# The last MLP block by chunks of 384 tokens, with each chunk's tail behind it, in a two-layer hybrid trunk

## The chip, the cores and the metric

The kernel runs on one core of one Trainium2 chip. Its engines are TensorE (PE in the rows, with its weight loads as PEld), VectorE (DVE), ScalarE (ACT), GpSimd (POOL) and SyncE (SP), whose queue issues the DMA transfers. The metric is the device time of one execution in microseconds, the median of several runs; lower is better. The time before is 3880.99 us (three runs, 3868.97 to 3885.31).

## The reference

Two layers over 1152 tokens of width 1024: 1024 latent tokens and 128 context tokens, which take their own modulation. A layer is

```python
h = rms_norm(x, g_pre_mix) * (1.0 + sc1) + sh1
o = mixer(h)        # one input projection, four head groups, one output projection
x = x + gt1 * rms_norm(o, g_post_mix)
h = rms_norm(x, g_pre_mlp) * (1.0 + sc2) + sh2
m = square(relu(h @ mlp_w1)) @ mlp_w2        # 1024 -> 4096 -> 1024
x = x + gt2 * rms_norm(m, g_post_mlp)
```

All is float32. The mixer's four groups (latent attention, windowed attention, a gated delta scan, a long convolution) are not touched here.

## The kernel before

**Numbers in two parts.** A float32 product is made of three matmuls (`mm3`, L213): every operand is split into a high half in the type fp32r (written by ACT) and a low half, the difference (`lo_of`, L232, on DVE), and high times high, high times low and low times high are added in PSUM. `load_cols` and `load_rows` load a weight, split it and leave both halves in SBUF.

**Tiles.** Tokens are nine tiles of 128 (tile 8 is the context). The normalised input of a projection lies transposed in sixteen tiles hT, eight of high and eight of low halves, each 128 features x 1152 tokens; `NCH` cuts their columns in three chunks of 384 tokens, that is three tiles each.

**The MLP** (`mlp`, L1786) goes over 16 blocks of two hidden tiles j. A block loads and splits w1 and w2 of both. For each chunk and j, 24 matmuls make hid (128 hidden x 384 tokens) in PSUM; ACT takes its ReLU (L1802), DVE multiplies it by itself (L1803), ACT writes the high half uh (L1804) and DVE the low half ul. When all chunks are done, each token tile t and half of the 1024 outputs takes six matmuls into mo, and DVE adds mo to acc (L1820): 18 accumulators of 128 x 512.

**The tail** (`tail`, L2132) of token tile t: `post` takes the sum of squares of acc (ACT, L449, two halves), rstd (two small DVE operations and a pow on POOL, L269), acc times rstd and gate (DVE, L1768), plus x (POOL, L1769); x is loaded from the scratch tensor xres, and the result is stored there, or to the output in layer 1. After layer 0, `rows` (L455) takes squares and rstd of the new row again and scales it in place, one half on ACT (L458), the other on DVE (L459), once the store has read it. `norm_transpose` makes hT of three such tiles: 24 transposes on PE into ht, ACT applies the modulation (L478), DVE casts to the high half (L480), DVE or POOL makes the low one (L482). Layer 0's tails run at the start of the next call of `layer`, tile by tile, behind `first_weights`, woven with `proj_first`, the first projection (48 columns with weights wb, and a tile of 128 with wah and wal; 48 matmuls for each chunk). Layer 1's tails run at the end.

**Pools and order.** SBUF tiles come from pools (L312): A and B with twelve buffers of 1152 float32 a partition, C with five and D with four, T with four of 512 for arriving weights, L with eight and H with six of 512. `self.big` is A in layer 0 and B in layer 1; acc takes nine of its twelve buffers. The first weights take six buffers of L, x of a tail two. A tile that is asked for gets a buffer that is free or will be next, and waits for that one's last reader. The order of instructions on each engine and on the DMA queue is fixed when the program is built: a scheduler goes over the program with a model of the timeline and packs it. Each engine then works through its list in order and waits where it must.

Of the kernel before, what the change touches and what calls it, by code (L numbers as in the profile page):

```python
# [11 lines left out]
F32R = mybir.dt.float32r  # L12
I32 = mybir.dt.int32
BF16 = mybir.dt.bfloat16
AF = mybir.ActivationFunctionType
ALU = mybir.AluOpType
# [3 lines left out]
DEPTH = 2  # L20
# [10 lines left out]
NCH = ((0, 384), (384, 384), (768, 384))  # L31
# [132 lines left out]
class Trunk:  # L164
# [294 lines left out]
        self.nc.vector.tensor_scalar(out=x[1], in0=x[1], scalar1=r, scalar2=None, op0=ALU.mult)  # L459
        return x  # L460

    def norm_transpose(self, tags, A, B, psum="Q"):

        nc = self.nc
        out = [self.W(dt=F32R, name="hT", tag=t) for t in tags]
        hi, lo = out[0::2], out[1::2]

        def group(g, xs):
            o = 384 * g
            sl = slice(o, o + 384)  # L470
            for k in range(8):
                pt = self.P(name="ht", tag=psum)
                for j in range(3):
                    self.tr(pt[:, j * 128:(j + 1) * 128], xs[j][k // 4][:, (k % 4) * 128:(k % 4) * 128 + 128])
                h = self.H(name="h")
                for c, a, b in ((0, 0, 384 if g < 2 else 256), (1, 256, 384)):
                    if c == 0 or g == 2:
                        nc.scalar.activation(out=h[:, a:b], in_=pt[:, a:b], func=AF.Identity,  # L478
                                             bias=B[:, k, c:c + 1], scale=A[:, k, c:c + 1])
                nc.vector.tensor_copy(out=hi[k][:, sl], in_=h[:, :384])  # L480
                E = nc.gpsimd if k % PL == PL - 1 else nc.vector
                E.tensor_tensor(out=lo[k][:, sl], in0=h[:, :384], in1=hi[k][:, sl].bitcast(F32), op=ALU.subtract)  # L482
                yield
        return hi, lo, group
# [1301 lines left out]
    def mlp(self, l, hi, lo):  # L1786
        nc = self.nc
        acc = []
        for b in range(16):
            us, w1s, w2s = [], [], []  # L1790
            for j in (2 * b, 2 * b + 1):
                w1s.append(self.load_cols(self.I["w1"][l, j], "w1"))
                w2s.append(self.load_rows(self.I["w2"][l, j * 128:(j + 1) * 128], "w2", [self.small] * 2))
                us.append((self.W(dt=F32R, name="uh", tag=self.big), self.W(dt=F32R, name="ul", tag="C" if j % 2 else self.big)))
            for c0, n in NCH:
                s = slice(c0, c0 + n)
                for w1, (uh, ul) in zip(w1s, us):
                    ps = self.P(name="hid", tag="Q")
                    for k in range(8):
                        self.mm3(ps[:, :n], w1(k), [hi[k][:, s], lo[k][:, s]], k == 0, k == 7)  # L1800
                    r = self.H(name="relu")
                    nc.scalar.activation(out=r[:, :n], in_=ps[:, :n], func=AF.Relu)  # L1802
                    nc.vector.scalar_tensor_tensor(out=r[:, :n], in0=ps[:, :n], scalar=0.0, in1=r[:, :n], op0=ALU.max, op1=ALU.mult)  # L1803
                    nc.scalar.copy(out=uh[:, s], in_=r[:, :n])  # L1804
                    self.lo_of(ul[:, s], r[:, :n], uh[:, s])
                if b == 0 and c0 < 768:
                    yield
            if b == 0:
                acc = [self.W((1024,), name="acc", tag=self.big) for _ in range(9)]
            for t in range(9):  # L1810
                ts = slice(t * 128, t * 128 + 128)
                for n in range(2):
                    ns = slice(512 * n, 512 * n + 512)
                    ps = self.P(name="mo")
                    for j in range(2):
                        self.mm3(ps, [x[:, ts] for x in us[j]], [x[:, ns] for x in w2s[j]], j == 0, j == 1)
                    if b == 0:
                        nc.vector.tensor_copy(out=acc[t][:, ns], in_=ps)
                    else:
                        nc.vector.tensor_tensor(out=acc[t][:, ns], in0=acc[t][:, ns], in1=ps, op=ALU.add)  # L1820
            yield acc

    def first_weights(self, l):

        nc = self.nc
        st = self.H((8, 48), name="wb", tag="T")
        nc.sync.dma_start(out=st, in_=self.I["wb"][l])
        w = [self.H((8, 48), F32R, name="wb", tag="L") for _ in range(2)]
        nc.scalar.copy(out=w[0], in_=st)
        self.lo_of(w[1], st, w[0])  # L1830
        return w, self.load_cols(self.I["wa"][l, 2], "wa")
# [163 lines left out]
    def layer(self, l):  # L1995


        I, nc = self.I, self.nc
        R = [["A"] * 12 + ["C"] * 4, ["B"] * 12 + ["D"] * 4]
# [5 lines left out]
        if l == 0:  # L2005

            xs = []
# [26 lines left out]
        if l == 0:  # L2034
            early = filters(self.gdn_tag, "Q", self.sines)
            with self.tc.issue_after(self.lead.ins):
                next(early)
        hi, lo, group = self.norm_transpose(R[0], *self.pre_scale(l, 0), "Q")
        if l == 0:
            with self.tc.issue_after(self.lead.ins):  # L2040
                self.more_consts()
        step, end = self.proj_first(l, hi, lo, w)
        for q in range(3):
            rows = xs[3 * q:3 * q + 3] if l == 0 else [self.rows(self.tail(t)) for t in range(3 * q, 3 * q + 3)]
            self.run((group(q, rows), 1), (step(q - 1) if q else iter(()), 2))
        self.run((step(2), 1))
        gab, gcw, head = end()
        g, be = self.gdn_shared(l, gab, self.gdn_tag)
# [45 lines left out]
        op = self.out_proj(l, R[1])  # L2094
# [7 lines left out]
        gate, xs = {}, []  # L2102
        A, B = self.pre_scale(l, 1)
# [10 lines left out]
        for ts in range(7):  # L2114
            g = op([ts])
            out = next(g)
            self.run((g, 1))
            finish([ts], out)
        hi, lo, group = self.norm_transpose(R[1], A, B)
        g = op([7, 8])  # L2120
        out = next(g)
# [6 lines left out]
        acc = next(g)  # L2128
        self.run((g, 1))
        gate2 = {}  # L2130

        def tail(t):  # L2132
            c = 0 if t < 8 else 1
            if c not in gate2:
                gate2[c] = self.gate_tile(l, 1, c, "H")
            y = [acc[t][:, 0:512], acc[t][:, 512:1024]]
            self.post(y, self.load_x(t, self.xres, "L"), gate2[c], y)
            if l + 1 < DEPTH:
                self.store_x(self.xres[t * 128:(t + 1) * 128], y)
            else:  # L2140
                self.store_x(self.O["y_s"][0, t * 128:(t + 1) * 128] if t < 8 else self.O["y_p"][0], y)
            return y
        self.tail = tail
        if l + 1 == DEPTH:
            for t in range(9):
                tail(t)


def run_timed(*gens):
# [42 lines left out]
```

## Time and profile before

| | us |
|---|---|
| median of three runs | 3880.99 |
| the profiled execution | 3886.4 |
| its span, first to last instruction | 3884.3 |
| PE busy | 3592.5 (92%) |
| DVE busy | 2267.7 (58%) |
| ACT busy | 1356.6 (35%) |
| POOL busy | 855.1 (22%) |
| between the layers, 1920.5 to 2004: PE busy | 52.35 of 83.5 |
| after the last matmul | 18.0 |

Busy time is an average over stages with different limits. Whether a stage's work is hidden is read from its own stretch: what an engine does there and, where it stands idle, what ended the wait. In rows of the timeline the number in brackets is the idle time of the engine ahead of the row, and the arrow names what ended it. "x3" means that three instructions of one kind in a row are shown as one.

### The profile page before, as it was taken

The numbers are of one execution on the slowest core, as the hardware profiler recorded it, in microseconds if no ns is written. First come the engines' busy times: TensorE is split into PE (matmuls) and PEld (weight loads), VectorE is DVE, ScalarE is ACT, GpSimd is POOL, SyncE is SP. The second block draws the span as 40 slices with busy tenths as digits, with TensorE's granted clock in tenths as the row PEclk, the third lists the DMA queues.
The fourth block names the chain that finished last, engine by engine and source line by source line (L and its number), as shares of the span: only waits on it lengthen the run. The fifth ranks groups of instructions, "written<-read, shape, count | busy, mean of one in ns | idle before, by whom it ended". The sixth has DMA issues, their size and how long they took to land. (4 is left out here: it accounts for less than half of the span.)

```text
span 3884.3 us, 57351 instructions
## 1 busy us (share of the span) xinstructions
PE 3592.5 (92%) x21674; PEld 3028.9 (78%) x21674; DVE 2267.7 (58%) x4583; ACT 1356.6 (35%) x2932; POOL 855.1 (22%) x806
## 2 busy tenths in 40 slices
PE   7989888899999999999979888878999999999997
PEld 4879764476789999999868887546677899999996
DVE  5665577686654444444566573778755544444446
ACT  5434333265542222221354334324544422222212
POOL 1152521264420000000221633214533200000003
PEclk9989888887999999999989898887859999999999
DMA  5355476741421111111234365864314211111113
GB/s 199 113 126 150 150 264 202 222 98 30 156 71 50 44 44 44 44 41 41 79 118 142 96 165 153 263 200 118 87 32 135 74 49 44 44 44 44 42 41 114
DMA packets 366399, 405.30 MB, mean 104 GB/s; under 512 B 116007, under 2 KB 237349, under 8 KB 366122
## 3 DMA queue, kind: packets, MB, share of 16 engines
q1 hardware_dynamic: 366122, 401.64, 33.7%
q8 instruction: 170, 2.79, 0.3%
q14 instruction: 107, 0.88, 0.1%
HBM read 298.34 MB, written 103.19 MB: 103 GB/s over the span
## 5 line engine op out<-in xcount | busy, mean ns | idle before, releaser
L213 PE MATMUL hid<-hT,w1h 128*128 128x384 f32 x3072 | 786.1, 335 | 0.1
L1820 DVE TENSOR_TENSOR acc<-acc,mo 128x512 f32<-128x512 f32 x540 | 370.1, 687 | 395.6 <-PE mo L213 395.5
L213 PE MATMUL pj<-hT,wah 128*128 128x384 f32 x2112 | 579.9, 352 | 11.7 <-ACT hc L516 8.6
L213 PEld LDWEIGHTS hid<-hT,w1h 128*128 128x128 f32 x3072 | 557.4, 188 | 13.7 <-ACT h L478 1.1
L213 PE MATMUL hid<-hT,w1l 128*128 128x384 f32 x1536 | 514.0, 335 | 0.0
L213 PE MATMUL mo<-w2h,uh 128*128 128x512 f32 x1152 | 451.8, 392 | 2.6 <-DVE acc L1820 2.6
L213 PE MATMUL mo<-w2l,uh 128*128 128x512 f32 x1152 | 451.3, 392 | 0.0
L213 PE MATMUL mo<-w2h,ul 128*128 128x512 f32 x1152 | 450.8, 392 | 0.0
L213 PEld LDWEIGHTS pj<-hT,wah 128*128 128x128 f32 x2112 | 398.0, 197 | 25.4 <-ACT hc L516 9.5
L659 POOL TENSOR_TENSOR e<-e,e 128x512 f32<-128x512 f32 (+1 forms) x216 | 307.1, 1423 | 318.2 <-ACT e L648 174.8
L269 POOL TENSOR_TENSOR postr<-postr,mhalf 128x1 f32<-128x1 f32 x36 | 22.1, 616 | 1604.9 <-DVE postr L268 1604.0
L213 PE MATMUL pj<-hT,wal 128*128 128x384 f32 x1056 | 369.4, 350 | 0.7 <-DVE wal L232 0.7
L242 ACT CAST w2h<-w 128x512 fp32r<-128x512 f32 x128 | 70.3, 619 | 732.9 <-PE mo L213 728.8
L213 PEld LDWEIGHTS hid<-hT,w1l 128*128 128x128 f32 x1536 | 288.2, 188 | 2.3
L232 DVE TENSOR_TENSOR el<-e,eh 128x512 fp32r<-128x512 f32 (+1 forms) x252 | 250.0, 1013 | 21.7 <-ACT eh L650 19.4
L213 PEld LDWEIGHTS mo<-w2h,ul 128*128 128x128 f32 x1152 | 216.6, 188 | 47.7
L213 PEld LDWEIGHTS mo<-w2h,uh 128*128 128x128 f32 x1152 | 216.6, 188 | 43.4 <-DVE acc L1820 3.1
L213 PEld LDWEIGHTS mo<-w2l,uh 128*128 128x128 f32 x1152 | 216.7, 188 | 39.4
L1803 DVE SCALAR_TENSOR_TENSOR relu<-hid,relu 128x384 f32<-128x384 f32 x192 | 106.1, 554 | 184.5 <-ACT relu L1802 184.5
L213 PEld LDWEIGHTS pj<-hT,wal 128*128 128x128 f32 x1056 | 207.6, 197 | 4.8 <-issue 2.0
L232 DVE TENSOR_TENSOR wal<-wa,wah 128x512 fp32r<-128x512 f32 x88 | 69.1, 787 | 173.3 <-ACT wah L253 139.2
L1802 ACT ACTIVATE relu<-hid 128x384 f32<-128x384 f32 x192 | 93.8, 488 | 202.8 <-PE hid L213 202.8
(488 smaller groups left out, 6392.5 us busy)
## 6 DMA issues: line engine op xcount, KB each, us to landing
w<-in_w SPq DMA_DIRECT2D x256, 256.0 KB
wada<-in_w_ada SPq DMA_DIRECT2D x192, 256.0 KB
wa<-in_wa SPq DMA_DIRECT2D x88, 256.0 KB
x<-in_x SPq DMA_DIRECT2D x18, 512.0 KB
Q<-rscr SPq DMA_DIRECT2D x32, 288.0 KB
o<-oscr SPq DMA_DIRECT2D x18, 512.0 KB
xres<-x SPq DMA_DIRECT2D x36, 256.0 KB
x<-xres SPq DMA_DIRECT2D x36, 256.0 KB
```

The lines of the kernel that those rows point to most:

```text
L213: self.last = self.nc.tensor.matmul(out, l, r, start=start, stop=stop, skip_group_check=True)
L232: self.nc.vector.tensor_tensor(out=lo, in0=x, in1=hi.bitcast(F32), op=ALU.subtract)
L242: self.nc.scalar.copy(out=hi[:, q], in_=st)
L269: self.nc.gpsimd.tensor_tensor(out=out, in0=out, in1=self.bcs(self.mhalf[:out.shape[0]], out.shape), op=ALU.pow)
L659: self.nc.gpsimd.tensor_tensor(out=acc, in0=acc, in1=e, op=ALU.add)
L1802: nc.scalar.activation(out=r[:, :n], in_=ps[:, :n], func=AF.Relu)
L1803: nc.vector.scalar_tensor_tensor(out=r[:, :n], in0=ps[:, :n], scalar=0.0, in1=r[:, :n], op0=ALU.max, op1=ALU.mult)
L1820: nc.vector.tensor_tensor(out=acc[t][:, ns], in0=acc[t][:, ns], in1=ps, op=ALU.add)
```

## The change

The MLP's loop stops after 15 blocks. The last block is a new function, `mlp_last`: it loads and splits the two hidden tiles' weights once and then goes chunk by chunk. A chunk makes its hid and u (one tile uc of three halves in the big pool and one in H) and at once the output products of its three token tiles; when a chunk's sums are complete, the three tails follow, and in layer 0 also `rows`. x of tiles 0 to 5 comes from the big pool, of 6 to 8 from L. The gate of the latent tokens moves to pool C, that of the context to L. Layer 1's hT is written into the tiles that held the MLP's input of layer 0, and its group 0 is made at the end of layer 0's call; `first_weights` comes behind all that.

```diff
     def mlp(self, l, hi, lo):
         nc = self.nc
         acc = []
-        for b in range(16):
+        for b in range(15):
...
+    def mlp_last(self, l, hi, lo, acc):
+
+        nc = self.nc
+        w1s, w2s = [], []
+        for j in (30, 31):
+            w1s.append(self.load_cols(self.I["w1"][l, j], "w1"))
+            w2s.append(self.load_rows(self.I["w2"][l, j * 128:(j + 1) * 128], "w2", [self.small] * 2))
+        for q, (c0, n) in enumerate(NCH):
+            s = slice(c0, c0 + n)
+            u = self.W((3, 384), F32R, "uc", self.big)
+            us = (u[:, 0], u[:, 1]), (u[:, 2], self.H((384,), F32R, "ul"))
+            for w1, (uh, ul) in zip(w1s, us):
+                ps = self.P(name="hid", tag="Q")
+                for k in range(8):
+                    self.mm3(ps[:, :n], w1(k), [hi[k][:, s], lo[k][:, s]], k == 0, k == 7)
+                r = self.H(name="relu")
...
+                nc.scalar.copy(out=uh, in_=r[:, :n])
+                self.lo_of(ul, r[:, :n], uh)
+                yield
+            for i in range(3):
+                for h in range(2):
+                    ns = slice(512 * h, 512 * h + 512)
+                    ps = self.P(name="mo")
+                    for j in range(2):
+                        self.mm3(ps, [x[:, 128 * i:128 * i + 128] for x in us[j]], [x[:, ns] for x in w2s[j]], j == 0, j == 1)
+                    nc.vector.tensor_tensor(out=acc[3 * q + i][:, ns], in0=acc[3 * q + i][:, ns], in1=ps, op=ALU.add)
+                yield q if i == 2 else None
...
-        hi, lo, group = self.norm_transpose(R[0], *self.pre_scale(l, 0), "Q")
+        hi, lo, group = self.norm_transpose(R[0], *self.pre_scale(l, 0), "Q") if l == 0 else self.ahead
...
+        else:
+            xs = self.rows_ahead
         step, end = self.proj_first(l, hi, lo, w)
-        for q in range(3):
-            rows = xs[3 * q:3 * q + 3] if l == 0 else [self.rows(self.tail(t)) for t in range(3 * q, 3 * q + 3)]
-            self.run((group(q, rows), 1), (step(q - 1) if q else iter(()), 2))
+        for q in range(l, 3):
+            self.run((group(q, xs[3 * q:3 * q + 3]), 1), (step(q - 1) if q else iter(()), 2))
...
-                gate2[c] = self.gate_tile(l, 1, c, "H")
+                gate2[c] = self.gate_tile(l, 1, c, "LC"[c == 0])
...
-            self.post(y, self.load_x(t, self.xres, "L"), gate2[c], y)
+            self.post(y, self.load_x(t, self.xres, self.big if t < 6 else "L"), gate2[c], y)
...
-        self.tail = tail
-        if l + 1 == DEPTH:
-            for t in range(9):
-                tail(t)
+
+        self.rows_ahead = []
+        if l + 1 < DEPTH:
+            self.ahead = self.norm_transpose(None, *self.pre_scale(l + 1, 0), "Q", (hi, lo))
+        for q in self.mlp_last(l, hi, lo, acc):
+            if q is not None:
+                y = [tail(t) for t in range(3 * q, 3 * q + 3)]
+                if l + 1 < DEPTH:
+                    self.rows_ahead += [self.rows(x) for x in y]
+                    if q == 2:
+                        self.run((self.ahead[2](0, self.rows_ahead[:3]), 1))
```

Three places show how the lists move; lines of the new program are numbered some 3 to 40 higher. Before, this stands on the DMA queue where layer 0's tails begin: the gate, and x of the tiles in halves (x_17337 is tile 0's first half, x_17365 tile 1's), each behind a store of the tile before.

```order
L440 DMA gate_17333<-grow 128x512
L440 DMA gate_17334<-grow 128x512
L1776 DMA x_17337<-xres 128x512
L1776 DMA x_17338<-xres 128x512
L1784 DMA xres<-acc_11560 128x512
L1776 DMA x_17365<-xres 128x512
L1784 DMA xres<-acc_11560 128x512
L1776 DMA x_17366<-xres 128x512
L1784 DMA xres<-acc_11561 128x512
```

In the new program the same place holds the weights' loads, and whole x tiles (x_17079, x_17095, x_17111 and x_17267 are tiles 0 to 3, x_17455 the first half of tile 6):

```order
L1860 DMA wb_17607<-in_wb 128x384
L440 DMA gate_17076<-grow 128x512 x2
L251 DMA wa_17613<-in_wa 128x512
L251 DMA wa_17619<-in_wa 128x512
L251 DMA wa_18100<-in_wa 128x512
L1782 DMA x_17079<-xres 128x1024
L1782 DMA x_17095<-xres 128x1024
L1787 DMA xres<-acc_11560 128x512
L1782 DMA x_17111<-xres 128x1024
L1787 DMA xres<-acc_11560 128x512
L1787 DMA xres<-acc_11561 128x512
L1779 DMA x_17455<-xres 128x512
```

Two x tiles are now asked for ahead of the first store, and x of tile 6 ahead of that of tile 3.

On DVE before, where the last hidden products of layer 0's MLP are split (ul), the additions of mo to acc follow with nothing of a tail between:

```order
L1803 SCALAR_TENSOR_TENSOR relu_17114<-hid_17089,relu_17114 128x384
L232 TENSOR_TENSOR ul_16944<-relu_17114,uh_16943 128x384
L232 TENSOR_TENSOR wal_17309<-wa_17305,wah_17307 128x512
L1803 SCALAR_TENSOR_TENSOR relu_17144<-hid_17119,relu_17144 128x384
L1820 TENSOR_TENSOR acc_11560<-acc_11560,mo_17149 128x512
L232 TENSOR_TENSOR ul_16968<-relu_17144,uh_16967 128x384
L1820 TENSOR_TENSOR acc_11560<-acc_11560,mo_17157 128x512
```

In the new program this stands on DVE between chunk 0 and chunk 1 of layer 0's last block (acc_11560 to acc_11562 are token tiles 0 to 2; L1771 is the product with rstd and gate, uc_17157 and ul_17158 are the low halves of chunk 1's u):

```order
L1771 SCALAR_TENSOR_TENSOR acc_11560<-acc_11560,postr_17085,gate_17076 128x512 x2
L451 TENSOR_TENSOR postr_17101<-postss_17098 128x1
L268 TENSOR_SCALAR postr_17101<-postr_17101 128x1
L1853 TENSOR_TENSOR acc_11562<-acc_11562,mo_17060 128x512
L1853 TENSOR_TENSOR acc_11562<-acc_11562,mo_17068 128x512
L1771 SCALAR_TENSOR_TENSOR acc_11561<-acc_11561,postr_17101,gate_17076 128x512 x2
L232 TENSOR_TENSOR uc_17157<-relu_17184,uc_17157 128x384
L451 TENSOR_TENSOR postr_17117<-postss_17114 128x1
```

The low half that chunk 1's output products read comes behind the gate products of tiles 0 and 1.

The third place is the low half of wb, the first weight of layer 1's projection. Before, it stands on DVE amid the last block's hidden products:

```order
L232 TENSOR_TENSOR ul_16944<-relu_17054,uh_16943 128x384
L1803 SCALAR_TENSOR_TENSOR relu_17084<-hid_17059,relu_17084 128x384
L232 TENSOR_TENSOR ul_16968<-relu_17084,uh_16967 128x384
L232 TENSOR_TENSOR wb_17296<-wb_17293,wb_17295 128x384
L232 TENSOR_TENSOR wal_17303<-wa_17299,wah_17301 128x512
```

In the new program it stands behind the gate products of the last three tiles and five casts of hT:

```order
L1771 SCALAR_TENSOR_TENSOR acc_11566<-acc_11566,postr_17463,gate_17076 128x512 x2
L1771 SCALAR_TENSOR_TENSOR acc_11567<-acc_11567,postr_17481,gate_17076 128x512 x2
L1771 SCALAR_TENSOR_TENSOR acc_11568<-acc_11568,postr_17503,gate_17491 128x512
L1771 SCALAR_TENSOR_TENSOR acc_11568<-acc_11568,postr_17503,gate_17492 128x512
L483 CAST hT_10945<-h_17634 128x384
L483 CAST hT_10947<-h_17649 128x384
L483 CAST hT_10949<-h_17663 128x384
L483 CAST hT_10951<-h_17677 128x384
L483 CAST hT_10953<-h_17691 128x384
L232 TENSOR_TENSOR wb_17610<-wb_17607,wb_17609 128x384
L485 TENSOR_TENSOR hT_10946<-h_17634,hT_10945 128x384
```

It has moved from ahead of all tails to behind the last one's gate product.

## Rows read from the trace of the kernel before

**Rows 1.** Three stretches: start:end, us, then busy time of each engine, granted clock.
```profile
1845.00:1895.00 50.00, 50.00 (x255) 45.53 (x254) 23.69 (x38) 10.18 (x20) 0.00 (x0) 1.00 0.13 41
1920.50:2004.00 83.50, 52.35 (x242) 42.66 (x242) 44.08 (x95) 47.35 (x110) 33.63 (x33) 0.71 0.30 102
2100.00:3000.00 900.00, 785.25 (x5692) 621.74 (x5691) 598.21 (x1310) 368.58 (x839) 343.75 (x325) 0.84 0.48 140
```
**Rows 2.** Waits of PE, 1895 to 2004: total us, times, longest.
```profile
PE ht L229 <- ACT acc L458: 28.0, 5, 6.5
```
**Rows 3.** Timeline of the DMA queue, layer 0's tails: start, us, what.
```profile
1905.34 0.43 SPq L1776 DMA_DIRECT2D x<-xres  x1
...
1922.77 0.43 SPq L1776 DMA_DIRECT2D x<-xres  x1
```
**Rows 4.** Timeline of PE and POOL at the end of layer 1.
```profile
3858.88 0.50 PE L213 MATMUL mo<-w2h,uh 128*128 128x512 f32 x1 [2.64 <-DVE acc L1820]
...
3865.88 0.40 PE L213 MATMUL mo<-w2h,ul 128*128 128x512 f32 x1
...
3875.05 6.20 POOL L1769 TENSOR_TENSOR acc<-x,acc 128x512 f32<-128x512 f32 x4 [0.40 <-issue]
```
**Rows 5.** Timeline of PE: hidden and output products, then four transposes.
```profile
3817.23 0.51 PE L213 MATMUL hid<-hT,w1h 128*128 128x384 f32 x2
...
3836.99 0.39 PE L213 MATMUL mo<-w2h,uh 128*128 128x512 f32 x1
...
3855.85 0.39 PE L213 MATMUL mo<-w2h,ul 128*128 128x512 f32 x1
...
1918.51 0.60 PE L229 MATMUL ht<-ident,acc 128*128 128x128 f32 x4
1918.87 0.47 PE L213 MATMUL mo<-w2h,uh 128*128 128x512 f32 x1
```
**Rows 6.** Groups by line, 1895 to 2004: count | busy us, mean ns | idle before.
```profile
L1769 POOL TENSOR_TENSOR acc<-x,acc 128x512 f32<-128x512 f32 x18 | 26.6, 1498 | 8.3 <-DVE acc L1768 5.5 <-PE mo L213 1.8 <-PE ht L229 0.9
L449 ACT ACTIVATE sqj<-acc 128x512 bf16<-128x512 f32 x36 | 22.6, 628 | 35.8 <-POOL acc L1769 34.3 <-DVE acc L1820 1.2
L480 DVE CAST hT<-h 128x384 fp32r<-128x384 f32 x24 | 12.9, 547 | 5.3 <-ACT h L478 5.3
L1820 DVE TENSOR_TENSOR acc<-acc,mo 128x512 f32<-128x512 f32 x18 | 11.9, 682 | 2.4 <-PE mo L213 2.3
L459 DVE TENSOR_SCALAR acc<-acc,prer 128x512 f32<-128x512 f32 x9 | 5.1, 568 | 10.0 <-DMA xres<-acc 9.8 <-POOL prer L269 0.2
L269 POOL TENSOR_TENSOR postr<-postr,mhalf 128x1 f32<-128x1 f32 x9 | 5.0, 550 | 755.2 <-DVE postr L268 755.2
L451 DVE TENSOR_TENSOR postr<-postss 128x1 f32<-128x1 f32 x9 | 2.2, 249 | 2.9 <-ACT sqj L449 2.9
```
**Rows 7.** Timeline of ACT and PE: last ReLU of layer 0, second chunk of layer 1.
```profile
1895.05 0.49 ACT L1802 ACTIVATE relu<-hid 128x384 f32<-128x384 f32 x1 [1.45 <-PE hid L213]
...
2003.96 0.62 PE L213 MATMUL pj<-hT,wah 128*128 128x384 f32 x2
```
**Rows 8.** Groups by line, whole run: two DVE operations of the hidden products.
```profile
L232 DVE TENSOR_TENSOR ul<-relu,uh 128x384 fp32r<-128x384 f32 x192 | 108.5, 566 | 88.3 <-ACT uh L1804 88.1
L1803 DVE SCALAR_TENSOR_TENSOR relu<-hid,relu 128x384 f32<-128x384 f32 x192 | 106.1, 554 | 184.5 <-ACT relu L1802 184.5
```
**Rows 9.** Timeline: PE after a wait; DVE alone, then beside POOL.
```profile
1925.31 3.42 PE L229 MATMUL ht<-ident,acc 128*128 128x128 f32 x13 [4.81 <-ACT acc L458]
...
1935.31 0.34 PE L213 MATMUL pj<-hT,wah 128*128 128x384 f32 x1
...
1918.61 1.42 DVE L1768 SCALAR_TENSOR_TENSOR acc<-acc,postr,gate 128x512 f32<-128x512 f32 x2
...
3874.17 4.75 DVE L1768 SCALAR_TENSOR_TENSOR acc<-acc,postr,gate 128x512 f32<-128x512 f32 x4 [1.49 <-POOL postr L269]
...
3850.30 1.27 DVE L1820 TENSOR_TENSOR acc<-acc,mo 128x512 f32<-128x512 f32 x2
```

More of the change, by code (lines that the diff above doesn't have):

```diff
@@ L460, in rows, with norm_transpose @@
         return x
-    def norm_transpose(self, tags, A, B, psum="Q"):
+    def norm_transpose(self, tags, A, B, psum="Q", out=None):
         nc = self.nc
-        out = [self.W(dt=F32R, name="hT", tag=t) for t in tags]
-        hi, lo = out[0::2], out[1::2]
+        if out is None:
+            t = [self.W(dt=F32R, name="hT", tag=t) for t in tags]
+            out = t[0::2], t[1::2]
+        hi, lo = out
         def group(g, xs):
@@ L1821, in mlp @@
             yield acc
+    def mlp_last(self, l, hi, lo, acc):
[13 more added lines that the diff above has]
+                r = self.H(name="relu")
+                nc.scalar.activation(out=r[:, :n], in_=ps[:, :n], func=AF.Relu)
+                nc.vector.scalar_tensor_tensor(out=r[:, :n], in0=ps[:, :n], scalar=0.0, in1=r[:, :n], op0=ALU.max, op1=ALU.mult)
+                nc.scalar.copy(out=uh, in_=r[:, :n])
[9 more added lines that the diff above has]
+                yield q if i == 2 else None
     def first_weights(self, l):
```

## The prediction

> **What bounds the kernel now.** I read the stretches around the change first [rows 1]. In an ordinary MLP block TensorE (PE) is busy all 50 us at a granted clock of 1.00, so there a change can only cost. Between the layers (1920.5 to 2004) it is busy 52 of 83.5 us at a mean clock of 0.71.
>
> Why it waits there stands in its waits: 28.0 us in five waits of transposes for ACT's row scaling (L458) [rows 2]. That ends a tile's tail: squares, rstd, VectorE (DVE) times gate, GpSimd (POOL) add, store, squares, scale. On the DMA queue a tile's x is loaded 8.7 us after the last one's (17.4 for two steps) [rows 3], just after the last tile's store: of pool L's eight buffers six hold the next layer's weights, so one x is in flight at a time. Nine tails in turn take some 80 us, of which the last block's products cover the first 25. At the end the same tail runs after the last product: products stop for 2.64 us, the last starts at 3865.88, the last POOL adds run to 3881.25 [rows 4], and 3.05 us of store follow to the span's end.
>
> **The change, step by step.** Products, bytes and evictions stay: 144 hidden and 108 output matmuls. A hidden one starts every 0.173 us (114 from the first row to the second), an output one every 0.227 (83 from the second to the third) [rows 5]; a chunk of 384 tokens is 48 x 0.173 + 36 x 0.227 = 16.5 us of PE. What moves is that the tails of chunks 0 and 1 come beside the products of chunks 1 and 2. Their x comes from three buffers of the big pool and is not one in flight any more; a tail's stages then follow POOL: a pow of 0.55 and two adds of 1.50 [rows 6], 3.6 us, about 5 with the DVE step between.
>
> Start of the new order, layer 0. Before, the last hidden product ends just ahead of the ReLU at 1895.05 [rows 7], say 1894.9. In the new order 96 hidden matmuls are still to do when chunk 0's are done, at 1894.9 - 96 x 0.173 = 1878.3.
>
> Step 1, to the last output product: 16.6 + 24.5 + 25 transposes of 0.09 (four in 0.36 at full clock [rows 5]) = 43.4, plus waits. The waits come from DVE. In a chunk it has six adds of 0.68, two ReLU products of 0.55, two low halves of 0.57, six gate products (0.71 alone, 1.67 beside a POOL add [rows 9]; I take 1.2), three row scalings of 0.57 and some 12 small ones of 0.25: 18.2 us for 16.5 of PE [rows 6, 8]. Behind chunk 1 come group 0's eight casts of 0.55 and six low halves, 7.8 us, ahead of the adds that free PSUM for tile 8. I take 6 us of waits (0 if the stages interleave perfectly, 13 if all is serial). Last product: 1927.7, seven later than before.
>
> Step 2, to the first weights of layer 1. They are now allocated behind x of tiles 6 to 8 in pool L, and DVE makes the low half of wb behind six gate products and five casts; before, this was done ahead of the tails. So: 2.5 us for the last adds in the queue, 1.3 for two squares, 1.3 for rstd with its pow, to 1932.8; six gate products alternating with POOL's six adds, 5 x 1.67 + 0.7 and a start of 0.5, to 1942.4; five casts and the low half, 3.3, to 1945.7. PE has only transposes meanwhile.
>
> Step 3: 168 projection matmuls (144 of the first step, 24 of the next tile) x 0.173 = 29.1, 27 transposes 2.4. PE restarts after a long wait. Before, after the wait of 4.81 us that ended at 1925.31, a projection matmul of 384 columns was down to 0.34 us, that of the hidden ones, by 1935.31 [rows 9]: about 9.5 us at 1.2 instead of 2.4 GHz, which cost 4.8. Sum: 1982.0. Before, PE reaches the same place, the second chunk of the next tile, at 2003.96 [rows 7]. Gain 22 us. Tiles 6 to 8 are scaled some 9 us after the weights, behind 48 matmuls that PE then has, so they cost nothing; without that cover up to 5.
>
> By the rows, four gate products beside four POOL adds take 7.08 us from the first start to the last end, 1.67 a pair [rows 4, 9]; alone they are 0.71 and 1.50, together 8.8. The Trainium skill (SBUF — State Buffer, "SBUF: two separate sides") has the port pair that VectorE and GpSimd share as an exclusive lock for a whole instruction, which speaks against laying these tails over each other. By that rule six pairs would take 13 us instead of 9 and the time would be some 5 us longer. The trace shows the stretching but not the full sum, and adds out of PSUM stay at 0.63 beside POOL [rows 9].
>
> End of layer 1. No rows follow, so DVE has some 14 to 15 us per chunk and I cost waits at nothing (bound 6). The last product ends at 3837.0 + 24.5 + 0.2 = 3861.7 instead of 3866.3. From there: tile 8's add and POOL's second pow 2.0, four adds at 1.68, then tile 8's pow, gate product and two adds, 4.5: 13.2, and the store 3.05: 3877.9 instead of 3884.3. Gain 6.4 (bounds 0 and 10).
>
> What follows layer 1's start is packed anew, and some of its mixer stands in another order. PE is busy 785 of 900 us there at clock 0.84 [rows 1], so it can win or lose. I take nothing, bounds 8 either way.
>
> **Sum.** -22 - 6.4 = -28 on an execution of 3886.4 us (span 3884.3 and 2.1 around it). The median shown is 3881.0, 5.4 lower; so 3853.
>
> **Rivals.**
> *More gain.* The chunk queues interleave and the clock stays up: the 6 and 4.8 us of losses go, and with a little more at the end the time is 3838. The limit, PE never waiting between the layers, is 1878.3 + 76.7 (all its work there) = 1955, 49 us of gain and 3826. For it speaks that x is ready early; against it the DVE sum. The range's lower end lies between.
> *DVE becomes the bound.* If every DVE operation with operands in SBUF pays the price beside POOL (low halves and scalings 1.4, gate products 1.67), a chunk is 25.2 us of DVE in layer 0, 8.7 over PE: 26 us over three chunks, 20 more than in the sum, and 4 at the end: 3877, no difference. For it: the pairs above. Against: POOL adds are 9 us of each 16.5, so not all fall beside one.
> *Slower: the next chunk's u is caught behind the tail.* ACT writes the new u into a buffer that an x leaves, and on DVE its low half stands behind a tile's gate products, which wait for a pow that waits on POOL for the last tile's adds. If a tile's chain takes the 8.7 us of the rows before, three take 26, 9.6 more than PE has, at two chunk starts in each of two layers: 38 us, and each such wait drops the clock, 4 x 4.8 = 19: -28 + 57, so 3910. It decides from a wait of 2.2 us per start (4 x (2.2 + 4.8) = 28), a chain of 6.2 us per tile. Against it: the 8.7 us held the wait for x, and my count of the chain is 5.
>
> **Chances.** Forecast 0.44 (its own range 3843 to 3862); more gain 0.20; DVE the bound 0.26; slower 0.10. The range 3833 to 3874 leaves a tenth below and above each. About 0.5% is what a measurement of this kernel can tell from no change; below 3862 lie the first two: faster 0.64, same 0.26, slower 0.10.
>
> **What would show it.** In the profile after: the x loads of layer 0's tail no longer 8.7 us apart; PE's last output product of layer 0 some 7 us later than before, then one long wait that ends with the low half of wb on DVE, not five waits for L458; the place of 2003.96 near 1982; in the last 30 us no stop of the products, and about 16 us after the last instead of 18. I am wrong if output products of chunks 1 and 2 wait for u by more than 2 us each, if the clock drops inside the block, or if what is won by 2004 is gone by 3000.

## The result, and the profile after

The changed kernel takes 3820.31 us (median of five runs, 3816.47 to 3831.28) against 3879.15 of the kernel before: a ratio of 0.9855, 95% interval 0.9825 to 0.9884. That is 59 us faster. Forecast were 28 (3853, range 3833 to 3874): the sign is right, the size is half of what came, and the time lies below the range. The profiled execution has a span of 3818.4 us, PE busy 3535.5 us (93%) and a mean granted clock of 0.941 (0.925 before).

Stretches of the changed kernel that answer to [rows 1] (start:end, us, then busy time of PE, PEld, DVE, ACT, POOL, granted clock): an ordinary MLP block, the step between the layers from the last output product to the 168th projection product, and the mixer.

```profile
1795.00:1845.00 50.00, 50.00 (x255) 45.53 (x254) 24.04 (x39) 10.29 (x20) 0.00 (x0) 1.00 0.13 43
1922.30:1974.30 52.00, 39.61 (x226) 33.08 (x225) 37.23 (x73) 31.86 (x71) 20.38 (x18) 0.86 0.24 77
2100.00:3000.00 900.00, 773.96 (x5676) 613.08 (x5674) 598.91 (x1274) 379.11 (x874) 355.23 (x336) 0.88 0.47 141
```

The step has shrunk from 83.5 to 52 us, its clock is 0.86 instead of 0.71, and the mixer's clock has risen too. Waits of PE from 1900 to 1975, which answer to [rows 2] (total us, times, longest):

```profile
PE pj L213 <- DVE wb L232: 8.6, 1, 8.6
PE mo L213 <- DVE acc L1853: 2.1, 1, 2.1
PE ht L229 <- ACT acc L458: 2.1, 1, 2.1
PE mo L213 <- ACT uc L1844: 1.6, 1, 1.6
```

Five waits for L458 with 28.0 us have become one with 2.1; the longest is now the one for wb. On the DMA queue (for [rows 3]) x of tiles 0 and 1 is asked for together while chunk 0's products run, that of tile 2 as they end, and the loads stand no longer 8.7 us apart (the last row is tile 6's, in halves):

```profile
1870.52 1.32 SPq L1782 DMA_DIRECT2D x<-xres  x2
1885.93 0.32 SPq L1782 DMA_DIRECT2D x<-xres  x1
...
1906.96 0.86 SPq L1779 DMA_DIRECT2D x<-xres  x2
```

PE of the changed kernel between the layers, for [rows 7]: an output product of the last tile, the two starts of projection products, the 168th of them, and the first hidden product of layer 1.

```profile
1922.25 0.63 PE L213 MATMUL mo<-w2h,ul 128*128 128x512 f32 x1
...
1931.03 0.56 PE L213 MATMUL pj<-hT,wb 128*48 128x384 f32 x2 [1.31 <-ACT wb L1862]
1940.20 5.42 PE L213 MATMUL pj<-hT,wb 128*48 128x384 f32 x22 [8.61 <-DVE wb L232]
...
1974.30 0.33 PE L213 MATMUL pj<-hT,wal 128*128 128x384 f32 x1
...
3002.86 0.44 PE L213 MATMUL hid<-hT,w1h 128*128 128x384 f32 x1
```

DVE in that wait: six gate products beside POOL's adds, five casts, then the low half of wb that PE waits for.

```profile
1927.28 8.12 DVE L1771 SCALAR_TENSOR_TENSOR acc<-acc,postr,gate 128x512 f32<-128x512 f32 x6 [0.19 <-POOL postr L269]
1935.32 3.56 DVE L483 CAST hT<-h 128x384 fp32r<-128x384 f32 x5
1938.80 1.34 DVE L232 TENSOR_TENSOR wb<-wb,wb 128x384 fp32r<-128x384 f32 x1
```

And the end of layer 1, PE and POOL, for [rows 4]:

```profile
3802.90 0.39 PE L213 MATMUL mo<-w2h,ul 128*128 128x512 f32 x1
...
3805.20 5.96 POOL L1772 TENSOR_TENSOR acc<-x,acc 128x512 f32<-128x512 f32 x4
...
3812.58 2.87 POOL L1772 TENSOR_TENSOR acc<-x,acc 128x512 f32<-128x512 f32 x2 [0.92 <-issue]
```

To compare the kernels I cut the span at three products that both have: the first hidden product of layer 0's MLP (1120.03 before, 1113.69 after), the 168th projection product of layer 1, and the first hidden product of layer 1. The last two stand in the trace of before at:

```profile
2003.38 0.34 PE L213 MATMUL pj<-hT,wal 128*128 128x384 f32 x1
...
3062.26 0.44 PE L213 MATMUL hid<-hT,w1h 128*128 128x384 f32 x1
```

| us | before | after | gain | forecast |
|---|---|---|---|---|
| up to layer 0's MLP, the same lists | 1120.0 | 1113.7 | 6.3 | 0 |
| B: MLP of layer 0 and the step | 883.4 | 860.6 | 22.7 | 22 |
| M: mixer of layer 1 | 1058.9 | 1028.6 | 30.3 | 0, bounds 8 |
| E: MLP of layer 1 to the span's end | 822.1 | 815.6 | 6.5 | 6.4 |

The first line is scatter between two executions of the same instructions: over all the profiles below this part goes from 1104 to 1126 us. B and E came out as forecast to within a microsecond. The surplus is M, in which the change computes nothing differently. So the experiments ask what made the mixer faster.

Inside M all of it lies in one stage, the last attention stage; from the 168th product to the stage's first sT the two took 824.7 and 826.6 us. From its first sT to the first op product (sS, sC and sT are scores of window groups, sO their products with the values; op is the output projection) before and after read, in the columns used above:

```profile
2828.10:2944.80 116.70, 107.93 (x414) 80.77 (x413) 67.62 (x120) 55.62 (x115) 48.18 (x38) 0.66 0.15 44
```
```profile
2800.90:2886.20 85.30, 78.75 (x411) 61.85 (x411) 68.23 (x119) 56.58 (x118) 50.05 (x38) 0.90 0.21 61
```

They are nearly the same products (from the stage's first sS to op it is 611 in both), and PE is idle for 8.8 and 6.6 us. So of the 31.4 us of difference 2.2 are waits; 29.2 are busy time, at a granted clock of 0.66 and of 0.90.

### The profile page after: what moved, and what is told of

Read it like the earlier page. It is cut to its first block, busy times and chain, and to the rows that moved or that the text cites. A ratio compares the mean times of both kernels' runs of the same rounds, so it can differ in the third digit from the quotient of the medians.

```text
span 3818.4 us, 57318 instructions
## 1 busy us (share of the span) xinstructions
PE 3535.5 (93%) x21674; PEld 2988.0 (78%) x21674; DVE 2278.2 (60%) x4583; ACT 1349.5 (35%) x2930; POOL 857.7 (22%) x806
## 5 line engine op out<-in xcount | busy, mean ns | idle before, releaser
L1823 DVE TENSOR_TENSOR acc<-acc,mo 128x512 f32<-128x512 f32 x504 | 345.9, 686 | 391.9 <-PE mo L213 391.9
L213 PE MATMUL mo<-w2h,ul 128*128 128x512 f32 x1116 | 435.2, 392 | 0.0
L213 PE MATMUL mo<-w2h,uh 128*128 128x512 f32 x1080 | 422.8, 391 | 0.0
L213 PE MATMUL mo<-w2l,uh 128*128 128x512 f32 x1080 | 422.6, 391 | 0.0
L213 PEld LDWEIGHTS mo<-w2h,uh 128*128 128x128 f32 x1080 | 202.8, 188 | 37.5
L213 PEld LDWEIGHTS mo<-w2l,uh 128*128 128x128 f32 x1080 | 202.7, 188 | 36.5
L213 PE MATMUL ada<-wada,cst 128*32 128x512 f32 x384 | 138.2, 683 | 31.3 <-DMA wada<-in_w_ada 31.0
```

Source lines behind the costliest of these rows:

```text
L213: self.last = self.nc.tensor.matmul(out, l, r, start=start, stop=stop, skip_group_check=True)
```

## The experiments

All numbers are read as above, from the profiled execution of each kernel; medians and ratios (95% interval) are against runs of before on the same chip.

| kernel | B | M | sT to op | E | median | ratio |
|---|---|---|---|---|---|---|
| before | 883.4 | 1058.9 | 116.7 | 822.1 | 3879.2 | |
| after | 860.6 | 1028.6 | 85.3 | 815.6 | 3820.3 | 0.9855 (0.9825 to 0.9884) |
| e1 chunks in layer 1 alone | 882.8 | 1060.8 | 116.5 | 815.5 | 3882.2 | 0.9986 (0.9966 to 1.0007) |
| e2 chunks in layer 0 alone | 861.0 | 1034.4 | 87.8 | 820.6 | 3832.1 | 0.9863 (0.9831 to 0.9895) |
| e3 before, gate in C | 902.9 | 1045.1 | 92.6 | 820.9 | 3890.6 | 1.0012 (0.9987 to 1.0037) |
| e4 after, gates in H | 855.7 | 1076.6 | 116.5 | 815.5 | 3863.5 | 0.9933 (0.9908 to 0.9959) |
| e5 before, last stage a | 882.8 | 1072.3 | 119.3 | 822.0 | 3884.9 | 1.0032 (1.0005 to 1.0058) |
| e6 before, last stage b | 882.3 | 1045.5 | 110.0 | 820.8 | 3876.0 | 0.9992 (0.9965 to 1.0018) |
| e7 before, x in the big pool | 899.3 | 1047.5 | 101.1 | 820.8 | 3885.6 | 1.0008 (0.9981 to 1.0035) |
| e8 after, first weights ahead | 855.5 | 1051.3 | 105.9 | 816.5 | 3839.6 | 0.9896 (0.9870 to 0.9921) |
| e9 before, last stage of after | 882.8 | 1024.4 | 92.9 | 820.8 | 3850.8 | 0.9922 (0.9891 to 0.9953) |
| e10 after, last stage of before | 860.9 | 1069.1 | 116.5 | 815.6 | 3869.1 | 0.9951 (0.9927 to 0.9974) |
| e11 e8, last stage of after | 855.5 | 1031.1 | 85.1 | 816.6 | 3820.6 | 0.9851 (0.9823 to 0.9878) |
| e12 before, half of that order | 881.6 | 1034.6 | 93.1 | 820.8 | 3866.8 | 0.9938 (0.9908 to 0.9968) |

My theory: the change shifts what the planner sees, the planner packs the mixer anew, and the new order of the products decides the clock. Rivals: the scatter of executions, or the entry into the mixer with tiles 3 to 8 ready.

**e1, chunks in layer 1 alone.**

```diff
-        for b in range(15):
+        for b in range(15 if l == 1 else 16):
```
(and layer 0's tails at the start of layer 1, as before)

> The last block goes by chunks in layer 1 alone; layer 0's end, the step between the layers and the mixer of layer 1 have the lists of the kernel before, instruction for instruction. M is the time of layer 1's mixer, from the 168th projection product of the layer to the first hidden product of its MLP: 1058.9 us in the trace before, 1028.6 after; E is the time from there to the span's end: 822.1 before, 815.6 after. My sum: E 815.6, M unchanged, 6.5 us faster, 3872.6. Packing theory (the order of the mixer decides M): M 1051 to 1067. Rival, M is luck of the execution: M anywhere between 1028 and 1060 with the old list too.

E was 815.5, M 1060.8. In the profile the end pays its 6.6 us by itself, and M repeats with the old list to within 2 us. The median was 10 us above what was expected, 7 of which the runs of before beside it had too (3885.8), and the ratio (5 us) is not clear of no change.

**e2, chunks in layer 0 alone.**

```diff
-        for b in range(15):
+        for b in range(15 if l == 0 else 16):
```

> The last block goes by chunks in layer 0 alone; layer 1's end as before. The mixer of layer 1 has the list of the changed kernel, instruction for instruction. My sum for this part: the place of the 168th projection product 22 us earlier. Packing theory: M 1021 to 1036, so 3820.3 + 6.5 = 3826.8. Luck: M anywhere between 1028 and 1060, and the median some 15 us higher.

B 861.0 and M 1034.4, 6 more than in the other profile of this list; the median was 5 above what was expected. B repeats, and the list goes with the low M: scatter as the cause of 30 us falls. By the ratios the gains of e1 and e2, 5 and 53 us, add up to that of the whole change, 56.

**e3, the kernel before with one pool changed.**

```diff
-                gate2[c] = self.gate_tile(l, 1, c, "H")
+                gate2[c] = self.gate_tile(l, 1, c, "CH"[c] if l == 0 else "H")
```

> The kernel before with the latent gate of layer 0's tails in pool C instead of H, nothing by chunks. That leaves the step between the layers as it is, but the mixer of layer 1 is packed anew (about one product in six stands elsewhere). Packing theory: M leaves 1058.9 by 8 us or more, to either side, and the median goes with it: 3879 + (M - 1059), anything from 3845 to 3890. Rival, the mixer is faster because the chunks let it start with tiles 3 to 8 ready: nothing of that here, M 1051 to 1067 and 3873 to 3885.

M fell by 14 with no chunk in it, and the last stage came in the changed kernel's order from its first sT on (the same 409 products in a row): 92.6 us. The median didn't follow, since B lost 20: the gate's load waited 23 us for a buffer of C that the block's products still read, which put off all tails.

**e4, the changed kernel with its gates in H.**

```diff
-                gate2[c] = self.gate_tile(l, 1, c, "LC"[c == 0])
+                gate2[c] = self.gate_tile(l, 1, c, "H")
```

> The changed kernel with the gates of the tails in pool H as before. The chunks and the step between the layers stay, layer 1's mixer is packed anew, and stands nearer to the list of before than to that of the changed kernel. Packing theory: M goes up, to 1040 to 1065, and the median to 3832 to 3857. Rival, an entry with tiles 3 to 8 ready: M stays at 1021 to 1036, median 3813 to 3828.

M rose by 48 to 1076.6, more than expected, and the median missed its range by 6. The last stage, which the planner now put in the order of before, took 116.5 us, 31 more than in the changed kernel; the mixer ahead of its first sT lost 16. So the entry with tiles 3 to 8 ready does not make a mixer fast. By the ratio 26 us of gain were left.

**e5 and e6, the kernel before with another weave in the last stage.**

```diff
-            for _ in weave([(main, 1), (preps[i + 1], PR)] + ...
+            for _ in weave([(main, 1), (preps[i + 1], 1.5 if l and i == 4 else PR)] + ...
```
(e6: i == 3)

> The kernel before; in layer 1's last attention stage alone the scores of the second window group are woven 1.5 instead of 1.6 steps to one of the first. All lists are those of before up to that stage's first sT product; from there to the first op product the same products stand in another order. That stretch took 116.7 us in the trace before, 116.5 in both others with its list, and 85 to 93 in three with another. Theory, the order of these products decides the clock and with it the time: the stretch leaves 116.6 by 8 us or more, and M and the median go with it, to 3848 to 3878. Rival, the state in which the stage is entered decides: 113 to 120, median 3879 to 3892.

> The same with another order: 1.5 instead of 1.6 steps one job earlier, lists of before up to the first sS product, then the last stage in a third order. Order theory: the stretch from sT to op away from 116.6 by 8 us or more, M and the median with it. Rival, the entry decides: 113 to 120, median 3879 to 3892.

119.3 and 110.0 us: neither left 116.6 by the 8 us that I had asked for. e5 came as the rival had it, e6 as neither had it. They told nothing for the order. M went 13 us either way, 10 and 6 of it in parts with unchanged lists, which shows what one profile of M is worth. By the ratio e5 was 12 us slower (2 to 23), more than the 2.6 of its stage; why is open.

**e9 and e10, the orders exchanged.** The products of this stage have the same names in both programs, so TensorE can be made to take them in the other's order.

```diff
+        for n in want:                       # tile numbers in the other kernel's order
+            i = left[n].pop(0)
+            if last is not None:
+                self.tc.add_manual_dep(i, last.name, mybir.DependencyInfo(mybir.DependencyClass.NoSync, mybir.DependencyReason.DATA), reason="order")
+            last = i
```

> The kernel before, nothing by chunks; edges of order alone (no waits on semaphores of their own) make TensorE take the some 470 products of layer 1's last attention stage, first sS to last sO, in the order of the changed kernel. All that stands ahead of the stage is as before. Theory, the order of these products decides the clock there: sT to op falls from 116.6 to 85 to 93 us, M from 1059 to 1022 to 1036, the median from 3882 to 3846 to 3860, without any chunk. Rival, it is what goes ahead of the stage or the other engines' lists: M 1050 to 1067 and 3874 to 3890.

> The changed kernel with the products of layer 1's last attention stage in the order of the kernel before. Order theory: sT to op rises from 85 to 114 to 120 us, M from 1029 to 1053 to 1068, the median from 3820 to 3845 to 3859; what is left against before is the step between the layers and the end, 29 us. Rival: M stays at 1021 to 1040, 3813 to 3832.

The stage of e9, then of e10:

```profile
2816.10:2909.00 92.90, 87.41 (x411) 68.50 (x410) 68.85 (x118) 54.63 (x114) 48.44 (x38) 0.79 0.19 54
```
```profile
2817.00:2933.50 116.50, 108.96 (x415) 81.27 (x414) 68.13 (x120) 55.93 (x115) 46.24 (x38) 0.66 0.16 44
```

The kernel before, with this one stage reordered, is 30 us faster by the ratio (18 to 42; median 3850.8 of four runs; M 1024.4, the lowest of all). The changed kernel with the old order loses it: 116.5 us, M up by 40, just over its range, and the median 10 above its own. It keeps 19 us by the ratio, where B and E are worth 29 by the profiles; so it lost 37, 7 more than e9 gained, which the intervals allow. Of M's 40 us 31 lie from sT to op; the other 9 are no more than unchanged lists differed by in e5.

So the order of the stage carries the gain, in either program. What is exchanged is a little more than TensorE's order: the lists of VectorE and ScalarE inside the stage followed it. By the names in the traces 116 of 117 VectorE operations from sT to op stand in e9 as in the changed kernel, and all 119 in e10 as before. TensorE's order alone, against the other engines' old lists, was not tried. Nor is the order all: with the changed kernel's order from sT on the stage takes 92.6 to 93.1 us in the program of before (e3, e9, e12) and 85.1 to 87.8 in the new one (after, e2, e11).

**e12, half of the order.**

> The kernel before with the last attention stage's products in the old order up to the stage's first sT, and in the changed kernel's order from there on: which part of that order carries its time. If the later part alone does (sT, sO and the small den and rb among the second group's scores): sT to op 85 to 95 us, M 1022 to 1040, median 3846 to 3862. If it hangs on what is done ahead of the first sT: 108 to 120, M 1046 to 1068, median 3872 to 3890.

93.1 us and M 1034.6: the part from the first sT on carries it. The profiled execution is the fastest of ten, though, 23 us below their median. The median missed its range by 5, but the runs of before beside it were at 3889.1; by the ratio it is 24 us faster.

**e7, x early without chunks.**

```diff
-            self.post(y, self.load_x(t, self.xres, "L"), gate2[c], y)
+            self.post(y, self.load_x(t, self.xres, big if l == 0 else "L"), gate2[c], y)
```

> The kernel before, nothing by chunks, with x of layer 0's tails in whole tiles of the big pool (three buffers free) instead of halves in L (two free). B is the time from the first hidden product of layer 0's MLP to the 168th projection product of layer 1: 883.4 before, 860.6 after. If x, one tile in flight, sets the pace of the tails: 4 to 5 us a tile instead of 8.7, B 850 to 868, so that the chunks would not be needed for it. Rival, the chain of tail operations sets it: B 879 to 887. The mixer is packed anew, its last stage in an order of 270 products that no run has had; order theory: M at 1025 to 1050.

B got worse, 899.3. POOL's adds of the first tiles:

```profile
1922.87 2.48 POOL L1769 TENSOR_TENSOR acc<-x,acc 128x512 f32<-128x512 f32 x2 [21.55 <-DMA x<-xres]
...
1930.46 2.87 POOL L1769 TENSOR_TENSOR acc<-x,acc 128x512 f32<-128x512 f32 x2 [0.92 <-DVE acc L1768]
...
1938.18 2.87 POOL L1769 TENSOR_TENSOR acc<-x,acc 128x512 f32<-128x512 f32 x2 [0.92 <-PE ht L229]
```

x now waited for the block's last products (the big pool is full until then), so the first tail came late; and with x there, a tile still took 7.6 to 7.7 us. So x was worth about 1 us of the 8.7, and did not set the pace of a tail, as I had read [rows 3]. The rest I put down to the chain of a tail's operations in engine order, which no run tried by itself; in the changed kernel, where three tails go together, POOL's adds follow each other in 4.3 to 5.9 us. By its trace the chunks win because six of nine tails lie beside products: POOL's adds of tiles 0 to 5 run from 1883.7 to 1915.8, the products until 1922.9.

**e8 and e11, the first weights ahead of chunk 2's tails.**

```diff
             if q is not None:
+                if q == 2 and l + 1 < DEPTH:
+                    self.w_ahead = self.first_weights(l + 1)
```
(and x of all tiles from the big pool; e11 with the order of e9 too)

> The changed kernel with the first weights of layer 1 asked for ahead of chunk 2's tails (their six buffers of L then come ahead of x, which is taken from the big pool for all tiles). The low half of wb stands on DVE beside the products of chunks 1 and 2. Step 2 of my sum: PE's wait of 8.6 us for it goes, B 847 to 854 instead of 860.6. Rival, tiles 6 to 8 are late next: B 857 to 862. The mixer is packed anew: M at 1021 to 1077, and the median 3820 + (B - 860.6) + (M - 1028.6).

> The kernel with the first weights ahead of chunk 2's tails, with the last attention stage in the changed kernel's order. In the run without that order B was 855.5 (860.6 in the changed kernel), sS to op 170.9 us (141.9). Order theory: sS to op 142 to 152, M 1022 to 1033, the median 3839.6 less some 24, 3808 to 3822, the fastest of all here. Rival: M 1045 to 1055, 3832 to 3846.

PE of e8 in the step:

```profile
1948.64 0.56 PE L213 MATMUL pj<-hT,wb 128*48 128x384 f32 x1 [4.67 <-DVE hT L483]
```

The wait for wb is gone, as step 2 had it, but 4.67 us of it came back one step on, for a cast of the next chunk's hT behind the same six gate products: B gained 5 of the 8.6, and at 855.5 lies between the two ranges. e8 is still slower than the changed kernel, by its mixer. e11 puts the stage right (85.1 us) and takes 19 us off e8, yet is no faster than the changed kernel (0.9851 and 0.9855): its M and E took 3.6 of the 5 us back. No version here beats the change.

## Why the prediction was wrong

**Steps 1 to 3, between the layers: right.** From the first hidden product of layer 0's MLP the last output product ended 8.7 us later than before (7 forecast); from there to the end of wb's low half it was 17.3 us (18.0 forecast); from there to the second chunk of the next tile, which starts behind the 168th product, 34.3 (36.3). The low clock at the restart cost less than my 4.8: the 22 products of the first row after the wait took 5.42 us, at the pitch of 0.173 it would be 3.8. Chunk 2 waited 1.6 us for u, below the mark of the slow rival, and 2.1 for a sum. The clock did fall inside the block, one of my signs of being wrong, but only for its last eight products (0.63 us in the row of 1922.25, 0.39 at the full clock).

**Tiles 6 to 8: right.** PE did not wait for their scaling (the one wait for L458 was for the group of tiles 3 to 5). The six gate products took 8.12 us and POOL's six adds 9.44, where my pairs gave 9. The Trainium skill (SBUF — State Buffer, "SBUF: two separate sides") would have the two exclude each other, by my estimate 13 us (4 more than 9, not the 5 that I wrote). That estimate was too high, because I misread [rows 6]: the 1.50 us there is no add alone but a mean, in which each tile's first add runs beside a gate product. With no VectorE work beside it an add of the kernel before took 1.26 us (1951.00), so six pairs in turn are 6 x (0.71 + 1.26) = 11.8; the trace took 10.6 from the first gate product to the last add. The four pairs at the end of layer 1 before, which I took for stretching, alternate when they are read one by one:

```profile
3875.05 1.65 POOL L1769 TENSOR_TENSOR acc<-x,acc 128x512 f32<-128x512 f32 x1 [0.40 <-issue]
3875.50 1.75 DVE L1768 SCALAR_TENSOR_TENSOR acc<-acc,postr,gate 128x512 f32<-128x512 f32 x1
3876.66 1.71 POOL L1769 TENSOR_TENSOR acc<-x,acc 128x512 f32<-128x512 f32 x1
3877.17 1.75 DVE L1768 SCALAR_TENSOR_TENSOR acc<-acc,postr,gate 128x512 f32<-128x512 f32 x1
```

Each gate product ends 0.55 us after the add beside which it started (3877.25 after 3876.70), and each add some 1.12 us after the gate product beside which it started (3878.37 after 3877.25): 1.67 a pair. That agrees with an exclusion far better than my reading did; the forecast of this wait came out because it used the measured 1.67.

**The end of layer 1: right.** Last product to the span's end 15.5 us (16 forecast, 18.5 before), and no stop of the products in the last 30 us.

**My reason for the old pace: wrong, at no cost.** e7 shows that x one at a time did not set the 8.7 us. My chain of about 5 us a tile stood close to the 4.3 to 5.9 of the new trace.

**The step that failed is the term for the mixer:** "What follows layer 1's start is packed anew ... I take nothing, bounds 8 either way." It measured 30.3 us, and without it the time would have been within 3 us of the forecast. Zero was no bad middle: in the five new packings that the planner made (after, e3, e4, e7, e8) M goes from 1028.6 to 1076.6, 30 below the old one and 18 above, with a mean of 1050. It is the bound that failed. I had seen the clock of 0.84 and "it can win or lose", and had priced it like a wait. A stage in which the clock can go either way has to be priced by what it costs at each level: 900 us at 0.84 are 144 us of clock not granted, and the last stage alone goes from 116.7 to 85.3. The traces bear this out for the whole mixer: half of the time for which the clock stood at 0.50 in it is 107.5 us in the changed kernel, 145.1 before and 163.8 in e4, and M less this half is 905 to 921 us in all fourteen profiles. With bounds of 30 the forecast would have reached down to 3853 - 30 = 3823, and the whole range, 10 below that, past the time. That the packing came out on the fast side was luck: in e4, the same chunks with the gates left in pool H, it came out on the slow one.

**The rivals.** "More gain" has the nearest time, 3838, but not its reason: the losses between the layers did not go (B is the forecast's own). DVE as the bound and the caught u did not come.

## What to carry to other kernels

Where a planner packs the whole program, an edit in one place reorders stages hundreds of microseconds away; cut both traces at common products before crediting a gain to the edit, and give each repacked stage its own term. If such a stage runs at a clock between the two levels, its bounds are what it takes at either, not some waits. Exchanging the order of one stage by edges of order alone separates the edit from its side effect in two runs, and may be worth as much as the edit: here 30 us against 29. Look then at what the other engines' lists did, since they move with it.

## What the runs showed of the hardware

The granted clock can stay at the lower of its two levels (1.2 of 2.4 GHz) while PE is busy almost without a break. In before it fell at 2815.8 and rose at 2887.4; in after, at about the same place in the work, it fell at 2786.4 and rose at 2800.0. Stretches of before, and of after:

```profile
2815.80:2887.40 71.60, 70.89 (x218) 51.69 (x219) 37.50 (x83) 24.92 (x50) 18.44 (x15) 0.50 0.05 15
```
```profile
2786.40:2800.00 13.60, 11.87 (x30) 7.54 (x29) 9.11 (x22) 2.58 (x7) 3.23 (x3) 0.50 0.00 1
2800.00:2830.00 30.00, 30.00 (x166) 22.58 (x165) 24.99 (x53) 19.70 (x41) 15.43 (x14) 1.00 0.13 34
```

Ahead of both falls PE did small score products of 64 rows (sS, sC) between O products, with short waits; before, then after:

```profile
2813.48 0.50 PE L213 MATMUL O<-el,VA 128*128 128x512 f32 x1 [1.13 <-DVE el L232]
...
2814.75 0.33 PE L213 MATMUL sC<-sK,sQ 64*128 64x128 f32 x1
...
2816.14 0.80 PE L213 MATMUL O<-el,VA 128*128 128x512 f32 x1 [0.73 <-DVE el L232]
```
```profile
2784.06 0.50 PE L213 MATMUL O<-el,VA 128*128 128x512 f32 x1 [0.59 <-DVE el L232]
...
2784.72 0.32 PE L213 MATMUL sC<-sK,sQ 64*128 64x128 f32 x1
...
2785.76 0.50 PE L213 MATMUL O<-el,VA 128*128 128x512 f32 x1 [0.38 <-DVE el L232]
...
2796.34 2.91 PE L213 MATMUL ST<-Q,K 97*128 97x512 f32 x6
```

After's clock came back behind a run of nine ST products of 512 columns; in before the same run started at 2823.38 and the clock stayed down. The Trainium skill (TensorE: Matmul & The Clock Gate, "What's actually happening") says that activity releases the throttle; 70.89 busy us of 71.60 did not do so here.

It repeats with the order. In all these profiles the clock falls 6 to 17 us ahead of the stage's first sT. It then stayed at 0.50 for 71.7 us in before, e1 and e4 and 75.1 in e10, which have the old order; for 34.1 us in e3, e9 and e12, which have the new order from sT on in the program of before; and for 13.7 us in after and e11 and 20.5 in e2, which have it in the new program. In the other orders of e5 to e8 it was 75.1, 23.9, 34.1 and 34.1 us. Which feature of the order ends the stretch stays open: e9, e10 and e12 show that the order decides, in its part from the first sT on; what in that part was not tried, nor what makes 34.1 us into 13.7 with the same order on TensorE.
